# Depthwise-convolution taps in a hybrid SSD / conformer / HGRN2 layer pair: another density, at most two at a step, over a longer stretch of the program

## The chip, the cores and the metric

The program runs on one NeuronCore of a Trainium2 chip. The core has TensorE (PE in the rows; PEld is its weight load), VectorE (DVE), ScalarE (ACT), GpSimd (POOL) and SyncE (SP, which here issues weight loads). Each engine takes its own instructions strictly in the order in which they were written, and engines wait for each other by semaphores. The metric is the device time of one execution in microseconds (us), the median of several.

## What is computed

Two layers over 256 latent tokens and 256 context tokens of width 1024. Layer 0 has a combined input projection, a Mamba-2 scan in both directions beside a conformer convolution, one output projection and a mixture of experts; layer 1 has a gated recurrence (HGRN2) and another mixture of experts. The change lies in layer 0. What it moves is the conformer convolution, and around it stand the scan, its gate z and the output projection:

```python
def conformer_conv(v, gate, dw_w, dw_b, ln_g, ln_b, rows):
    u = v * jax.nn.sigmoid(gate)
    ...
    u = dwconv(u, dw_w, dw_b).reshape(b, n, ch)          # 31 taps, 1024 channels
    return jax.nn.silu(layernorm(u, ln_g, ln_b))

    # even_mixer
    o_ssd = ssd_readout(ys_l[0] + ys_l[1], xs_l, pl[..., :SSD_INNER], d_skip, ssd_g)
    o_cf = conformer_conv(pl[..., cf0:cf0 + CF_CH], pl[..., cf0 + CF_CH:], cf_w, cf_b, cf_lng, cf_lnb, rows)
    y_lat = (jnp.concatenate([o_ssd, o_cf.astype(o_ssd.dtype)], axis=-1) @ w_out).astype(hl.dtype)
```

## The kernel before

Channels lie on the 128 partitions in the input projection, so the 1024 conformer channels are eight blocks of 128, and a block holds all 512 tokens in its free dimension. A product of fp32 precision is made of three products of fp32r pieces: a weight piece is split by ScalarE (the high part, L478) and GpSimd or VectorE (the low part, L479) into a buffer `wb`, and a GEMM of one block takes 24 matmuls of 512 columns.

Blocks 0 to 4 of the conformer convolution run on TensorE. Blocks 5, 6 and 7 run on VectorE: `cf_evac` (L691) multiplies value and sigmoid gate into a padded tile `u` (L702, L703), and then puts 31 closures into the list `bgq`, one for each tap. A tap is one instruction of 572 columns on two accumulators `ca`: taps 0 and 1 are tensor-scalar products (L717, L719), taps 2 to 30 are `SCALAR_TENSOR_TENSOR` (L721), and the last one is followed by the two additions (L724, L725) that write the block's output `co[i]`, a quarter of a tile `um`. In all that is 93 taps and six additions.

Three stages of the program follow each other here.

- **The fill.** `states()` and `tiles_of()` run the scan as Python generators that interleave: `group(t, g)` makes the decay matrices `sb` (ScalarE L1093, GpSimd L1090), TensorE sums them, ScalarE takes the exponential `seg` (L1110), VectorE and GpSimd multiply it by `cb` into `sc` (L1117), and TensorE adds `y`. `states()` adds chunk states `S` (GpSimd L1056, VectorE L1060), `rest()` adds the carried part (VectorE `t` L1159, GpSimd `um` L1161). Between these, the list `FILL` writes the GEMMs of conformer blocks 5 to 7 and of the modulation.
- **The end of the recurrence.** When `FILL` is used up, `drain()` steps the generators until none is left, with no GEMM between them.
- **The z gates.** Eight GEMMs make z; `z_gate` (L1217) takes SiLU (ScalarE L1220), multiplies by the scan's result (VectorE L1225, four instructions), scales into the fp32r pair (ScalarE L1227, VectorE L1228), and squares for the norm (ScalarE L1231, GpSimd L1232). ScalarE's split of the weights of later z blocks (L478) stands in the same queue behind these. After the z gates TensorE sums the eight `co` blocks with `ones` (L1419, tile `y`) for the layer norm, and starts the output projection.

What sets the order of the taps is `step(us, rate)`. Each call runs the generators once, adds `us * rate` to a credit, capped at 6.0, and then writes one tap from `bgq` for each whole unit of credit. `cm_gemm` calls it twice for a GEMM, with 3.8 and 1.9 us, `mod_task` twice with 1.7 us. `RATE[0]` is 1.4 in the fill and in the z gates, and `drain()` calls `step()` without time, so it adds no credit. What is left in `bgq` is written behind the last z GEMM.

Of the kernel before, what the change touches and what calls it, by code (L numbers as in the profile page):

```python
# [89 lines left out]
def build(tc, I, out):  # L90
# [32 lines left out]

    live, pend = [], []
    bgq = []
    credit = [0.0]

    def begin(g):
        live.append(g)

    def step(us=0.0, rate=0.0):

        todo = list(pend)
        pend.clear()
        for f in todo:
            f()
        for g in list(live):
            if next(g, live) is live:
                live.remove(g)
        credit[0] = min(credit[0] + us * rate, 6.0)  # L140
        while credit[0] >= 1.0 and bgq:
            bgq.pop(0)[1]()
            credit[0] -= 1.0

    def drain():
        n = 0
        while live or pend:
            step()
            n += 1
            assert n < 500  # L150

# [7 lines left out]
    class Slots:  # L159
# [27 lines left out]
        def main(self, *a):  # L187

            n = 0
            while (x := self.now(*a)) is None:  # L190
                n += 1
                assert n < 500
                step()
            return x
# [287 lines left out]
    class Pieces:  # L482
# [26 lines left out]
        def next(self, keep=False):  # L509

            if not keep:
                self.release()
            self.ahead()
            v, r, b = self.ready.pop(self.pos)
            self.pos += 1
            self.held.append((r, b))
            return v
# [139 lines left out]
    cfp = stcf.enter_context(tc.tile_pool(name="cfp", bufs=1))  # L657


    RATE = [0.6]  # L660

    def bg(us):
        step(us, RATE[0])

# [162 lines left out]
    def mod_task(l, b, slots=ACC):  # L827
        acc = slots.main()
        for kh in range(2):
            mod_half(acc.ap, l, b, kh)  # L830
            bg(1.7)

        def g():
            sb = yield from TMP.take()
            SC.activation(sb.ap, acc.ap, AF.Copy)
            acc.done()
            yield
            p = yield from TRS.take()
            mod_cols(p.ap, sb.ap)
            sb.done()  # L840
            yield
            mod_add(p.ap, l, b)
            p.done()
            mods_done.add((l, b))
        pend.append(lambda: begin(g()))
# [143 lines left out]
    for i in range(8):  # L989
# [4 lines left out]
        for b in CF_AT.get(i, ()):  # L994
            cf_task(b)
    drain()
    stcf.close()
    st1.close()
# [179 lines left out]
    def tiles_of(pace):  # L1178
        n = 0
        for t in range(4):  # L1180
            begin(cb(t))
            for g in range(4):
                begin(group(t, g))
                nlive[0] += 1
                if g % 2:
                    begin(rest(t, g // 2))
                for _ in range(pace):
                    yield
                while nlive[0] > 3:
                    yield  # L1190

    begin(states())
    begin(tiles_of(3))
    RATE[0] = 1.4
    for f in FILL:
        if f[0] == "cvg":
            if f[2]:
# [2 lines left out]
                cm_task(lambda acc: PA.update(v=acc))  # L1200
        else:
            mod_task(f[1], f[2])
    drain()
    stack_s.close()


# [45 lines left out]
        flags.add("rso")  # L1252

    flags = set()
    RATE[0] = 1.4
    for i in range(8):
        cm_task(lambda acc, i=i: begin(z_gate(i, acc)))
    begin(z_norm())
# [247 lines left out]
    for part in (0, 1):  # L1506
# [4 lines left out]
        for hf in range(2):  # L1511
# [24 lines left out]
            if part == 0 and hf == 1:  # L1536
                uo[0:4] = [unit(og, f"uo{i}") for i in range(4)]
                S.ring(uo[0:4], last=mod_last)
    drain()
    S.hold(True)  # L1540
    P.release()
# [1328 lines left out]
```

## Time and profile before

| | us |
|---|---|
| Median of 3 runs | 1563.47 |
| Lowest and highest | 1562.69, 1569.62 |
| Profiled execution | 1567.05 |
| Its span, first to last instruction | 1565.2 |

The page gives for the whole span TensorE 88% busy, VectorE 60%, ScalarE 48%, GpSimd 42%. These are averages over stages with different limits. The stages of the change lie between 280 and 530 us of the span: the fill from the first tap at about 280 to the last `sc` of it at 396.6, the end of the recurrence to 434.5, where the first z GEMM starts, the z gates to 482.4, then the output projection. How to read the rows: a line of the timeline gives start, length, engine, line, operation and tiles, the count, and in brackets the idle time ahead of it and what ended it. A line of groups gives the count, the busy time and mean length in ns, and behind the second bar the idle time ahead with its releaser.

### The profile page before, as it was taken

What the parts mean: (1) busy time and instruction counts of PE and PEld (TensorE: products, weight loads), DVE (VectorE), ACT (ScalarE), POOL (GpSimd) and SP (SyncE); (2) the same over time, 40 slices, a digit from 0 to 9 for tenths busy, and PEclk for the clock granted to TensorE, in tenths of its full rate; (3) what the DMA queues carried; (4) which work ended last, traced back from release to release, by engine and by line L of the source; (5) the groups of instructions that cost most, each with busy time, mean ns of one, the idle gap of its engine ahead of it and who ended that gap; (6) DMA issues with size and microseconds to landing.
All of it is one profiled execution on the core that took longest, in us unless ns stands there. A gap on an engine that the chain in (4) does not pass through costs nothing. (4 is left out here: it accounts for less than half of the span.)

```text
span 1565.2 us, 19174 instructions
## 1 busy us (share of the span) xinstructions
PE 1383.8 (88%) x7144; PEld 920.0 (59%) x7144; DVE 937.0 (60%) x1268; ACT 755.2 (48%) x1269; POOL 653.7 (42%) x408
## 2 busy tenths in 40 slices
PE   5999989796698988799999994799999988999995
PEld 2677755454476665576666772677777765433432
DVE  2665540899397466789999882634645655132223
ACT  4453435363535534578887882644444553212222
POOL 4333324787855374356667552333233324000000
PEclk9999999898899999899999997799999998999998
DMA  9266443553024164899999995422212466899994
GB/s 332 86 153 153 121 117 135 162 189 107 2 66 150 54 215 155 292 372 374 373 373 333 346 372 210 164 82 79 80 56 81 170 261 273 366 420 420 420 421 172
DMA packets 154311, 340.56 MB, mean 218 GB/s; under 512 B 8105, under 2 KB 45233, under 8 KB 141408
## 3 DMA queue, kind: packets, MB, share of 16 engines
q1 hardware_dynamic: 147440, 323.69, 58.2%
q0 software_dynamic: 5504, 11.79, 2.4%
q10 hardware_dynamic: 1264, 3.73, 0.7%
q8 instruction: 61, 1.00, 0.3%
q14 instruction: 42, 0.34, 0.1%
HBM read 332.79 MB, written 12.42 MB: 221 GB/s over the span
## 5 line engine op out<-in xcount | busy, mean ns | idle before, releaser
L479 POOL TENSOR_TENSOR wb<-wring,wb 128x1024 fp32r<-128x1024 f32 x68 | 170.1, 2504 | 275.4 <-ACT wb L478 232.5
L99 PE MATMUL acc<-hh,wb 128*128 128x512 f32 x640 | 207.3, 401 | 4.0 <-ACT wb L478 2.1
L478 ACT ACTIVATE wb<-wring 128x1024 fp32r<-128x1024 f32 x90 | 94.8, 1058 | 104.0 <-PE acc L99 57.3
L99 PEld LDWEIGHTS acc<-hh,wb 128*128 128x128 f32 x640 | 119.2, 188 | 39.1 <-issue 6.0
L99 PE MATMUL acc<-wb,um 128*96 128x512 f32 (+1 forms) x480 | 122.8, 402 | 5.9 <-DVE wb L479 2.9
L99 PE MATMUL acc<-hl,wb 128*128 128x512 f32 x320 | 126.9, 396 | 0.3 <-DVE hl L604 0.2
L721 DVE SCALAR_TENSOR_TENSOR ca<-u,pcol,ca 128x572 f32<-128x572 f32 x87 | 109.7, 1318 | 0.0
L99 PEld LDWEIGHTS acc<-wb,um 128*96 128x96 f32 (+1 forms) x480 | 79.2, 169 | 38.7 <-DVE wb L479 6.0
L99 PE MATMUL y<-hu,hu 128*64 128x512 f32 (+2 forms) x296 | 85.0, 519 | 4.6 <-DVE hu L2167 2.7
L2611 POOL DMA_INDIRECT hu<-hD,ig x7 | 7.1, 1010 | 172.4 <-DVE ig L2610 154.4
L479 POOL TENSOR_TENSOR um<-wring,um 128x1024 fp32r<-128x1024 f32 x17 | 53.8, 3166 | 55.3 <-ACT um L478 53.1
L2659 DVE TENSOR_TENSOR sg<-sg,y 64x512 f32<-64x512 f32 x16 | 11.1, 692 | 106.8 <-ACT sg L2658 106.8
L99 PE MATMUL acc<-um,um 128*96 128x512 f32 (+2 forms) x272 | 69.1, 394 | 2.8 <-POOL um L479 2.8
L99 PEld LDWEIGHTS acc<-hl,wb 128*128 128x128 f32 x320 | 60.1, 188 | 15.2 <-DVE hl L604 1.6
L479 DVE TENSOR_TENSOR wb<-uo,wb 128x1024 fp32r<-128x1024 f32 x32 | 60.6, 1928 | 9.8 <-ACT wb L478 9.5
L99 PE MATMUL acc<-uo,um 128*96 128x512 f32 (+1 forms) x240 | 62.9, 400 | 0.0
L479 POOL TENSOR_TENSOR um<-uo,um 128x1024 fp32r<-128x1024 f32 x18 | 50.2, 2790 | 26.4 <-ACT um L478 26.3
L873 DVE SCALAR_TENSOR_TENSOR xa<-xin,pcol,xa 128x514 f32<-128x514 f32 x64 | 58.7, 918 | 2.3
L2658 ACT ACTIVATE sg<-y 64x512 f32<-64x512 f32 x16 | 9.4, 588 | 104.3 <-PE y L99 104.3
L99 PEld LDWEIGHTS y<-hu,hu 128*64 128x64 f32 (+2 forms) x296 | 31.5, 150 | 39.5 <-issue 33.6
L99 PEld LDWEIGHTS acc<-um,um 128*96 128x96 f32 (+1 forms) x272 | 43.6, 176 | 17.8 <-POOL um L479 5.7
L99 PE MATMUL acc<-wb,hxh 128*128 128x512 f32 x160 | 52.7, 411 | 0.0
(672 smaller groups left out, 3477.5 us busy)
## 6 DMA issues: line engine op xcount, KB each, us to landing
wring<-in_mod_w_dram SPq DMA_DIRECT2D x32, 1024.0 KB, 5.3
uo<-in_moe_w_down_dram SPq DMA_DIRECT2D x19, 1024.0 KB, 14.4
wring<-in_moe_w_gate_dram SPq DMA_DIRECT2D x16, 1024.0 KB, 13.7
hu<-in_moe_w_gate_dram SPq DMA_DIRECT2D x16, 1024.0 KB, 14.5
uo<-in_moe_w_up_dram SPq DMA_DIRECT2D x13, 1024.0 KB, 9.9
wring<-in_moe_w_up_dram SPq DMA_DIRECT2D x13, 1024.0 KB, 8.4
wring<-in_hg_w_in_dram SPq DMA_DIRECT2D x13, 1024.0 KB, 5.2
hu<-in_moe_w_down_dram SPq DMA_DIRECT2D x13, 1024.0 KB, 10.5
```

What stands on the lines that cost most here:

```text
L99: PE.matmul(o, l, r, start=start, stop=stop, skip_group_check=True)
L478: SC.activation(hv, w, AF.Copy)
L479: eng.tensor_tensor(lv, w, hv.bitcast(F32), op=ALU.subtract)
L721: DV.scalar_tensor_tensor(a, x, w, a, op0=ALU.mult, op1=ALU.add)
L873: DV.scalar_tensor_tensor(a[:, 0:514], x[:, k:k + 514], par("sc_w", 16 * k + i), a[:, 0:514], op0=ALU.mult, op1=ALU.add)
L2611: GP.indirect_dma_start(out=xg1[0:n], out_offset=None, in_=hD1[:, :], in_offset=bass.IndirectOffsetOnAxis(ap=ig[0:n, :1], axis=0), bounds_ ...
L2658: SC.activation(sv[up], av[0:CAP], AF.Silu)
L2659: DV.tensor_tensor(sv[up], sv[up], av[up], op=ALU.mult)
```

## The change

`RATE[0]` goes from 1.4 to 0.7 in both places, `step` writes at most two taps in a call, and the `drain` behind the fill gets 1.5 us for each of its steps, so that it writes taps too. Nothing else changes: the same 93 taps and six additions, the same instructions on all engines.

```diff
     live, pend = [], []
     bgq = []
+    RATE = [0.6]
     credit = [0.0]
...
         credit[0] = min(credit[0] + us * rate, 6.0)
-        while credit[0] >= 1.0 and bgq:
+        n = 0
+        while credit[0] >= 1.0 and bgq and n < 2:
             bgq.pop(0)[1]()
             credit[0] -= 1.0
-
-    def drain():
+            n += 1
+
+    def drain(us=0.0):
         n = 0
         while live or pend:
-            step()
+            step(us, RATE[0])
             n += 1
             assert n < 500
...
-    RATE = [0.6]
...
-    RATE[0] = 1.4
+    RATE[0] = 0.7
     for f in FILL:
...
-    drain()
+    drain(1.5)
     stack_s.close()
...
     flags = set()
-    RATE[0] = 1.4
+    RATE[0] = 0.7
     for i in range(8):
         cm_task(lambda acc, i=i: begin(z_gate(i, acc)))
```

The order of instructions on TensorE, ScalarE, GpSimd and SyncE is the same in both kernels; only VectorE's differs. Three places of it follow. Line numbers are three higher in the kernel after up to L660, and two higher behind it.

VectorE in the last part of the fill, before: `S`, `sc` and `t` are the instructions that TensorE and GpSimd wait for, `ca` are the taps.

```order
L1073 TENSOR_TENSOR cb_2571<-acc_2572,mL 128x512
L721 SCALAR_TENSOR_TENSOR ca<-u,pcol,ca 128x572 x2
L1117 TENSOR_TENSOR sc<-seg,cb_2570 128x512
L436 TENSOR_REDUCE modc_166<-tr 128x8
L437 TENSOR_TENSOR modc_166<-modc_166,pcol 128x8
L721 SCALAR_TENSOR_TENSOR ca<-u,pcol,ca 128x572 x3
L1060 TENSOR_TENSOR S<-S,acc_2641 128x512
L721 SCALAR_TENSOR_TENSOR ca<-u,pcol,ca 128x572 x7
L1117 TENSOR_TENSOR sc<-seg,cb_2570 128x512
L1159 TENSOR_TENSOR t_2744<-acc_2720,sm_439 128x512
```

The same place after:

```order
L1075 TENSOR_TENSOR cb_2551<-acc_2552,mL 128x512
L723 SCALAR_TENSOR_TENSOR ca<-u,pcol,ca 128x572 x2
L1119 TENSOR_TENSOR sc<-seg,cb_2550 128x512
L439 TENSOR_REDUCE modc_166<-tr 128x8
L440 TENSOR_TENSOR modc_166<-modc_166,pcol 128x8
L723 SCALAR_TENSOR_TENSOR ca<-u,pcol,ca 128x572 x2
L726 TENSOR_TENSOR um_101<-ca 128x256
L727 TENSOR_TENSOR um_101<-ca 128x256
L1062 TENSOR_TENSOR S<-S,acc_2617 128x512
L719 TENSOR_SCALAR ca<-u,pcol 128x572
L721 TENSOR_SCALAR ca<-u,pcol 128x572
L723 SCALAR_TENSOR_TENSOR ca<-u,pcol,ca 128x572
```

Where 3 and 7 taps stood ahead of `S` and of `sc`, two stand now, with the end of block 5 and the two opening taps of block 6.

VectorE at the end of the recurrence, before:

```order
L1117 TENSOR_TENSOR sc<-seg,cb_2902 128x512 x2
L1159 TENSOR_TENSOR t_2996<-acc_2987,sm_439 128x512
L1159 TENSOR_TENSOR t_3027<-acc_3007,sm_439 128x512
L1117 TENSOR_TENSOR sc<-seg,cb_2902 128x512 x2
L1159 TENSOR_TENSOR t_3095<-acc_3086,sm_439 128x512
L1159 TENSOR_TENSOR t_3109<-acc_3106,sm_439 128x512
L721 SCALAR_TENSOR_TENSOR ca<-u,pcol,ca 128x572 x13
L1225 TENSOR_TENSOR uo_3125<-uo_3125,um_102 128x128 x2
```

The same place after:

```order
L1119 TENSOR_TENSOR sc<-seg,cb_2873 128x512
L723 SCALAR_TENSOR_TENSOR ca<-u,pcol,ca 128x572 x4
L1119 TENSOR_TENSOR sc<-seg,cb_2873 128x512
L1161 TENSOR_TENSOR t_2973<-acc_2963,sm_439 128x512
L723 SCALAR_TENSOR_TENSOR ca<-u,pcol,ca 128x572 x2
L1161 TENSOR_TENSOR t_3006<-acc_2985,sm_439 128x512
L723 SCALAR_TENSOR_TENSOR ca<-u,pcol,ca 128x572
L1119 TENSOR_TENSOR sc<-seg,cb_2873 128x512
L723 SCALAR_TENSOR_TENSOR ca<-u,pcol,ca 128x572 x3
L1119 TENSOR_TENSOR sc<-seg,cb_2873 128x512
L1161 TENSOR_TENSOR t_3078<-acc_3068,sm_439 128x512
L723 SCALAR_TENSOR_TENSOR ca<-u,pcol,ca 128x572 x2
```

Taps now stand between the last `sc` and `t`, where none stood; 16 of them in this stretch.

VectorE at the last two z gates, before (`uo_3125` holds z, `A_170` is a gain that is needed later):

```order
L1225 TENSOR_TENSOR uo_3125<-uo_3125,um_103 128x128 x2
L1228 SCALAR_TENSOR_TENSOR uo_3124<-uo_3125,pcol,uo_3122 128x512
L1225 TENSOR_TENSOR uo_3125<-uo_3125,um_102 128x128 x2
L1225 TENSOR_TENSOR uo_3125<-uo_3125,um_103 128x128 x2
L457 SCALAR_TENSOR_TENSOR A_170<-modc_166,pcol 128x16
```

The same place after (`um_101` holds the blocks 4 to 7 of the convolution's output):

```order
L1227 TENSOR_TENSOR uo_3113<-uo_3113,um_103 128x128 x2
L723 SCALAR_TENSOR_TENSOR ca<-u,pcol,ca 128x572 x2
L1230 SCALAR_TENSOR_TENSOR uo_3112<-uo_3113,pcol,uo_3110 128x512
L723 SCALAR_TENSOR_TENSOR ca<-u,pcol,ca 128x572 x2
L1227 TENSOR_TENSOR uo_3113<-uo_3113,um_102 128x128 x2
L1227 TENSOR_TENSOR uo_3113<-uo_3113,um_103 128x128 x2
L723 SCALAR_TENSOR_TENSOR ca<-u,pcol,ca 128x572 x4
L726 TENSOR_TENSOR um_101<-ca 128x256
L727 TENSOR_TENSOR um_101<-ca 128x256
L460 SCALAR_TENSOR_TENSOR A_170<-modc_166,pcol 128x16
```

Each of the first six gates now has two taps between its products and its L1228 and two behind that, and block 7 ends behind the seventh gate's products instead of ahead of the third's.

## Rows read from the trace of the kernel before

**Rows 1.** The page's first line: span and instructions.

```profile
span 1565.2 us, 19174 instructions
```

**Rows 2.** Stages: stretch, its length, busy PE, PEld, DVE, ACT, POOL, PEclk, DMA.

```profile
280.00:396.60 116.60, 88.77 (x504) 56.30 (x504) 112.28 (x116) 53.26 (x136) 95.84 (x76) 0.89 0.46 145
396.60:434.50 37.90, 28.22 (x177) 19.84 (x178) 12.16 (x18) 18.18 (x55) 28.81 (x27) 0.89 0.00 0
434.50:482.40 47.90, 45.82 (x197) 36.02 (x195) 44.56 (x54) 19.04 (x26) 27.56 (x12) 1.00 0.34 104
```

**Rows 3.** Waits of TensorE from 280 to 400 us: total us, times, longest.

```profile
PE y L99 <- DVE sc L1117: 10.2, 3, 5.4
PE acc L99 <- DVE S L1060: 5.1, 2, 3.9
...
PE y L99 <- DVE modc L436: 1.7, 1, 1.7
```

**Rows 4.** Timeline of TensorE in the fill.

```profile
349.82 1.10 PE L99 MATMUL y<-sc,xd 128*64 128x128 f32 x16
...
382.61 1.98 PE L99 MATMUL y<-sc,xd 128*64 128x128 f32 x16 [3.87 <-DVE sc L1117]
384.51 2.08 PE L99 MATMUL acc<-S,um 128*128 128x256 f32 x4
```

**Rows 5.** Groups of VectorE in the fill, 280 to 396.6 us.

```profile
L721 DVE SCALAR_TENSOR_TENSOR ca<-u,pcol,ca 128x572 f32<-128x572 f32 x61 | 80.8, 1381 | 0.0
```

**Rows 6.** Line L721 alone: shortest, median and longest tap in ns.

```profile
L721 DVE SCALAR_TENSOR_TENSOR ca<-u,pcol,ca x87: 793/1157/3011, 282.1 to 462.1; 128x572 f32<-128x572 f32 x87
```

**Rows 7.** Groups of GpSimd in the fill, 280 to 396.6 us.

```profile
L1105 POOL TENSOR_TENSOR xd<-um,sm 128x256 f32<-128x256 f32 x18 | 17.5, 993 | 0.0
...
L1090 POOL TENSOR_TENSOR sb1h<-mL,lah 128x512 fp32r<-128x512 f32 x9 | 13.3, 1483 | 0.0
...
L1161 POOL TENSOR_TENSOR um<-um,t 128x512 f32<-128x512 f32 x6 | 9.3, 1543 | 15.7 <-DVE t L1159 15.7
```

**Rows 8.** Groups of GpSimd at the recurrence's end, 396.6 to 434.5 us.

```profile
L1161 POOL TENSOR_TENSOR um<-um,t 128x512 f32<-128x512 f32 x6 | 8.1, 1352 | 2.2 <-DVE t L1159 2.2
...
L1105 POOL TENSOR_TENSOR xd<-um,sm 128x256 f32<-128x256 f32 x9 | 6.7, 762 | 0.0
L1090 POOL TENSOR_TENSOR sb1h<-mL,lah 128x512 fp32r<-128x512 f32 x4 | 4.2, 1038 | 0.0
```

**Rows 9.** Groups of VectorE at the recurrence's end, 396.6 to 434.5 us.

```profile
L1159 DVE TENSOR_TENSOR t<-acc,sm 128x512 f32<-128x512 f32 x6 | 4.1, 689 | 7.1 <-PE acc L99 7.1
L1117 DVE TENSOR_TENSOR sc<-seg,cb 128x512 f32<-128x512 f32 x5 | 3.6, 712 | 15.3 <-ACT seg L1110 15.3
```

**Rows 10.** Timeline of VectorE in the z gates.

```profile
431.43 14.82 DVE L721 SCALAR_TENSOR_TENSOR ca<-u,pcol,ca 128x572 f32<-128x572 f32 x13
446.17 0.88 DVE L1225 TENSOR_TENSOR uo<-uo,um 128x128 f32<-128x128 f32 x4
...
469.55 3.84 DVE L1225 TENSOR_TENSOR uo<-uo,um 128x128 f32<-128x128 f32 x4 [0.25 <-ACT uo L1220]
474.24 0.75 DVE L1228 SCALAR_TENSOR_TENSOR uo<-uo,pcol,uo 128x512 fp32r<-128x512 f32 x1 [0.86 <-ACT uo L1227]
475.24 3.88 DVE L1225 TENSOR_TENSOR uo<-uo,um 128x128 f32<-128x128 f32 x4 [0.25 <-ACT uo L1220]
```

**Rows 11.** Timeline of GpSimd in the z gates.

```profile
469.11 1.31 POOL L1232 TENSOR_TENSOR uo<-uo 128x512 f32<-128x512 f32 x1 [2.50 <-ACT uo L1231]
470.54 2.50 POOL L479 TENSOR_TENSOR wb<-wring,wb 128x1024 fp32r<-128x1024 f32 x1
```

**Rows 12.** Timeline of TensorE where the z gates end.

```profile
482.44 1.92 PE L99 MATMUL y<-um,ones 128*32 128x512 f32 x16
...
486.15 1.64 PE L99 MATMUL acc<-wb,uo 128*128 128x512 f32 x6
491.62 1.12 PE L469 MATMUL tr<-ident,modc 128*128 128x128 f32 x4 [3.83 <-ACT m2r L471]
```

## The prediction, made before the changed kernel was run

> **What bounds the kernel now.** I first read the span [rows 1] and then the stages around the moved taps [rows 2]. In the fill (280 to 396.6 us) VectorE is busy 112.28 of 116.6 us, GpSimd 95.84 and TensorE only 88.77, at a granted clock of 0.89. At the end of the recurrence (to 434.5) VectorE does 12.16 of 37.9 us, while GpSimd works 28.81. In the z gates TensorE is busy 45.82 of 47.9 at a clock of 1.00, and VectorE 44.56. So VectorE paces the fill, then stands nearly idle for a stage, and then is full again.
>
> The waits of TensorE in the fill [rows 3] name the instructions behind which it stands: `sc` 10.2 us, `S` 5.1, `modc` 1.7, together 17.0. None of these is long itself; they stand behind taps in VectorE's queue. 61 of the `SCALAR_TENSOR_TENSOR` taps run there at a mean of 1381 ns [rows 5]; with the six opening taps 67 of the 93 stand in the fill, and no row shows VectorE idle ahead of a tap. GpSimd waits for the same queue: 15.7 us ahead of its `um` for VectorE's `t` [rows 7]. Each long wait costs TensorE twice: the `y` products behind the 3.87 us wait took 1.98 us where the same sixteen took 1.10 elsewhere, and the next products 2.08 [rows 4], the mark of the lower of the two clock levels.
>
> **The fill.** Counted in the order of instructions, 40 taps stand in it after instead of 67, and at most four in a row instead of seven (most often two). 27 taps less at 1.381 us are 37 us of VectorE's 112.28, which leaves about 75 us of work: it is no longer the fullest engine. What can TensorE gain? Its waits are 17.0 us, and the low clock cost at most 88.77 x (1 - 0.89) = 9.8 us: 26.8 us if all of it went. What is late next is GpSimd, whose order is unchanged. It was idle 116.6 - 95.84 = 20.8 us in the fill, 15.7 of them behind `t`. Without quicker operations it can't end the stage more than 20.8 us sooner. I take **-18**, between 15.7 and 20.8, nearer to the first, since seven or so of the awaited instructions still find two taps ahead. If each of these cost the mean of one tap, 7 x 1.4 = 10 us of the 17.0 would stay, and with a little of the clock the gain would be 10. Bounds: -10 to -21.
>
> **The end of the recurrence.** 16 taps come here, 18.5 us at the median of 1157 ns [rows 6]. VectorE's idle time here is 15.3 us ahead of `sc` and 7.1 ahead of `t` [rows 9], and the taps stand in front of just these, four, two, one, three, two at a time, so for VectorE they mostly fit. They aren't free for GpSimd, though. The same operations on GpSimd are longer where VectorE is full: `sb1h` 1483 ns in the fill against 1038 here, `xd` 993 against 762, `um` 1543 against 1352 [rows 7, 8]. With the counts here that is 4 x 0.445 + 9 x 0.231 + 6 x 0.191 = 5.0 us if VectorE were as full as in the fill (96%). It goes from 32% to (12.16 + 18.5) / 37.9 = 81%, some three quarters of the way: 3.8 us. GpSimd is on the path here (28.81 of 37.9 busy, ScalarE's `seg` the other link), so I count **+4**. Bounds: 0 (its 9.1 us of idle time takes it in) to +9 (every one of 16 taps holds GpSimd up for its shortest 0.793 us, 12.7, less some of that idle time).
>
> The rows show GpSimd slowed beside VectorE, not stopped. The Trainium skill, "SBUF — State Buffer", section "Who interferes with whom", says that a VectorE instruction with two SBUF inputs contends with a GpSimd instruction that reads SBUF, and that one holds the port pair for its whole length while the other blocks. By that rule the sum would use the upper bounds here and in the next part.
>
> **The z gates.** I count from E, the start of the first z GEMM (434.5 before). Before, VectorE starts 13 taps at E - 3.1 and they take 14.82 us, 1.14 each [rows 10]. After, it has six taps and the two additions of block 6, then the two opening taps and one more of block 7: 7 x 1.14 + some 3.1 = 11.1, so the first gate's products start at E + 8.0 and end at E + 8.9 [0.88, rows 10], sooner than at 446.17 (E + 11.7) before. Then come six gates with four taps each. A gate without taps repeats every 5.69 us (469.55 to 475.24), of which 3.84 are the products, held up while GpSimd splits weights from 470.54 for 2.50 us [rows 10, 11]. That is the floor of a gate with taps. The ceiling is all in turn: VectorE 0.88 + 0.75 + 4 x 0.793 = 4.8, GpSimd 1.31 + 2.50 = 3.8 [rows 6, 10, 11], together 8.6. I take the middle, 7.2: the seventh gate's products end at E + 8.9 + 6 x 7.2 = E + 52.1. Four taps and two additions follow, 5.8 us: block 7 is ready at E + 57.9.
>
> Who waits for it? Before, block 7 ended ahead of the third gate. Now TensorE, in order, stands at the sums `y<-um,ones`, which it reached before at 482.44, E + 47.9 [rows 12], and behind these the output projection is queued. So this is a new wait of some 10 us. But TensorE stood at that place before as well: after two units of the output projection (1.64 each) it waited 3.83 us for ScalarE's `m2r` and went on only at 491.62, E + 57.1 [rows 12]. After, it goes on at E + 57.9 with the last of the sums (1.0), the two units (3.3) and the small ones still to do, some 4.4 us: 57.9 + 4.4 - 57.1 = **+5**. With a gate of 5.7 us the taps end 9 us sooner and the term is about -2 (the gates' own waits of TensorE, 47.9 - 45.82 = 2.1, go too); with 8.6 it is +14.
>
> **The sum.** -18 + 4 + 5 = -9 us. The profiled execution took 1567.05 us, with a span of 1565.2 [rows 1], and lies 3.6 above the median of 1563.47. 1567.05 - 9 = 1558; taken to the median, 1563.5 - 9 = **1554.5 us**. Behind 500 us nothing is changed, and no row says that a shift of 9 us would be lost.
>
> **The rivals.**
> - *The taps hide almost entirely* (-21 in the fill, 0 at the recurrence's end, -2 in the gates): -23, 1540 us. For it speaks VectorE's idle time of 15.3 and 7.1 us [rows 9]; against it the 3.84 us for products that take 0.88 alone [rows 10].
> - *GpSimd and ScalarE take over the fill.* Taps stay in front of the awaited instructions and GpSimd's 95.84 of 116.6 us hardly shrink: -10 + 4 + 5 = -1, 1562.5 us, no change. For it speaks that GpSimd is nearly as full as VectorE; against it, that 15.7 us of its idle time hang on `t`.
> - *Slower: block 7 becomes the end of the stage.* VectorE and GpSimd take turns, a gate needs 8.6 us, block 7 comes at E + 66.3, the gates cost +14, the recurrence's end +9, and the fill brings only 10: +13, 1576 us. With -10 and +4 for the other two, it decides from a gate of some 8.6 us on (-10 + 4 + 14 = +8). The page's rule named above would give this case; the trace agrees with it where one split stops the products (3.84 against 0.88), not in the fill, where both engines show over 80% busy.
> - *The change doesn't do what it says.* The order shows that it does; 0.02.
>
> **How the numbers follow.** Forecast within 5 us of 1554.5: 0.44. Hidden: 0.16. Fill taken over: 0.28. Slower: 0.10. A measurement of this kernel can tell about 0.5%, 7.8 us, from no change. Faster by more than that (below 1555.7) are all of the hidden case and about two thirds of the forecast, 0.46; within it the rest of the forecast and the third case, 0.45; slower 0.09. The range reaches from within the hidden case (1543) to 4 us above now (1567.5), which leaves out most of the slower case and a part of the hidden one.
>
> **What would show it.** In the profile after, TensorE's waits for `sc` and `S` in the fill should fall from 15.3 to under 6 us, its clock there rise from 0.89, and GpSimd's 15.7 us ahead of `um` shrink to a few. At the recurrence's end `sb1h` and `xd` should be longer than 1038 and 762 ns. In the gates the products L1225 should follow each other by about 7 us, and `y<-um,ones` should show a wait for VectorE of about 10 us, which the row before doesn't have. I am wrong if the fill is less than 10 us shorter, or if a gate repeats under 6 or over 8.5 us.

## The result, and the profile after

| | before | after |
|---|---|---|
| Median of 20 runs each, us | 1563.78 | 1555.05 |
| Ratio after / before, 95% interval | | 0.9929 [0.9916, 0.9941] |
| Span of the profiled execution | 1565.2 | 1552.2 |
| Fill: first tap to TensorE's last `y<-sc` of the stage | 116.4 | 93.7 |
| End of the recurrence, to the first z GEMM (E) | 37.6 | 43.7 |
| z gates, E to `rso` on VectorE | 67.8 | 73.6 |
| Block 7's last addition ends | E + 32.6 | E + 59.4 |

The kernel is 0.7% faster, 1555.05 against a forecast of 1554.5 us. One of the 20 executions after took 1966.87 us at a mean clock of 0.648; it counts in the median (1554.63 without it), and the ratio leaves it out. The stages come from the starts of four instructions in the timelines of one profiled execution each. They changed by -22.7, +6.1 and +5.8, together -10.8 us; the other 2.2 us of the span lie ahead of the first tap (-1.2) and behind `rso` (-1.0). The medians differ by 8.7 us and the profiled executions by 13.1, since the one before lay 3.3 us above its median and the one after 1.1 below.

The page's first line of the kernel after:

```profile
span 1552.2 us, 19176 instructions
```

The three stages after, with the columns of [rows 2]:

```profile
279.10:372.80 93.70, 80.52 (x504) 53.17 (x505) 77.75 (x85) 49.79 (x126) 85.22 (x73) 0.96 0.56 180
372.80:416.50 43.70, 29.02 (x176) 20.18 (x177) 37.16 (x36) 21.34 (x66) 39.69 (x30) 0.88 0.00 1
416.50:462.70 46.20, 46.20 (x194) 37.12 (x194) 43.05 (x53) 19.05 (x26) 26.71 (x12) 0.97 0.38 114
```

In the fill VectorE (third of the busy times) fell from 112.28 to 77.75 us and is no longer the fullest engine: GpSimd is, 85.22 of 93.7. TensorE's clock rose from 0.89 to 0.96. At the end of the recurrence VectorE and GpSimd, which did 12.16 and 28.81 us, are now busy for 37.16 and 39.69 of 43.7.

TensorE's waits in the fill after, 279 to 376 us, which answer to [rows 3] (total us, times, longest):

```profile
PE acc L99 <- DVE u L705: 2.4, 2, 1.4
PE y L99 <- DVE modc L439: 2.3, 1, 2.3
PE y L99 <- DVE sc L1119: 2.3, 2, 1.2
PE y L99 <- POOL um L1163: 2.2, 3, 1.0
PE acc L99 <- DVE S L1062: 2.1, 1, 2.1
PE y L99 <- POOL sc L1119: 1.8, 2, 1.4
PE acc L99 <- POOL xd L1043: 1.5, 2, 1.3
PE tr L99 <- POOL sb1h L1092: 0.3, 1, 0.3
```

The waits for `sc` and `S` went from 15.3 to 4.4 us. No wait is longer than 2.3 us, and four of the eight lines name GpSimd (POOL), with 5.8 of 14.9 us. GpSimd's groups in the fill after, which answer to [rows 7]:

```profile
L1107 POOL TENSOR_TENSOR xd<-um,sm 128x256 f32<-128x256 f32 x16 | 13.8, 878 | 0.0
...
L1092 POOL TENSOR_TENSOR sb1h<-mL,lah 128x512 fp32r<-128x512 f32 x8 | 11.3, 1411 | 0.0
...
L1163 POOL TENSOR_TENSOR um<-um,t 128x512 f32<-128x512 f32 x6 | 9.4, 1567 | 4.2 <-DVE t L1161 4.2
```

Its idle time behind `t` went from 15.7 to 4.2 us; `xd` went from 993 to 878 ns and `sb1h` from 1483 to 1411, while `um` stayed as it was (1543 and 1567). At the end of the recurrence, which answers to [rows 8], the same instructions went the other way, `um` from 1352 ns, `xd` from 762 and `sb1h` from 1038:

```profile
L1163 POOL TENSOR_TENSOR um<-um,t 128x512 f32<-128x512 f32 x6 | 10.1, 1686 | 2.6 <-DVE t L1161 2.6
L1107 POOL TENSOR_TENSOR xd<-um,sm 128x256 f32<-128x256 f32 x10 | 9.3, 953 | 0.0
L1092 POOL TENSOR_TENSOR sb1h<-mL,lah 128x512 fp32r<-128x512 f32 x5 | 7.2, 1444 | 0.0
```

One gate of the kernel after, VectorE's timeline (start, length); [rows 10] showed gates without taps:

```profile
450.83 0.88 DVE L1227 TENSOR_TENSOR uo<-uo,um 128x128 f32<-128x128 f32 x4
451.64 1.53 DVE L723 SCALAR_TENSOR_TENSOR ca<-u,pcol,ca 128x572 f32<-128x572 f32 x2
453.09 0.74 DVE L1230 SCALAR_TENSOR_TENSOR uo<-uo,pcol,uo 128x512 fp32r<-128x512 f32 x1
453.75 4.72 DVE L723 SCALAR_TENSOR_TENSOR ca<-u,pcol,ca 128x572 f32<-128x572 f32 x2
458.39 0.89 DVE L1227 TENSOR_TENSOR uo<-uo,um 128x128 f32<-128x128 f32 x4
```

GpSimd in the same gate:

```profile
453.13 1.85 POOL L1234 TENSOR_TENSOR uo<-uo 128x512 f32<-128x512 f32 x1 [2.83 <-ACT uo L1233]
454.95 2.91 POOL L482 TENSOR_TENSOR wb<-wring,wb 128x1024 fp32r<-128x1024 f32 x1
```

The two pairs are the same instructions. The first runs while GpSimd stands idle and takes 1.53 us; the second runs beside GpSimd's sum of squares and weight split and takes 4.72, to 0.6 us behind the split's end. A gate repeats after 7.56 us, and VectorE has no idle time in it. TensorE at the end of the z gates, which answers to [rows 12]:

```profile
463.26 1.92 PE L99 MATMUL y<-um,ones 128*32 128x512 f32 x14
475.93 1.91 PE L99 MATMUL y<-um,ones 128*32 128x512 f32 x2 [10.76 <-DVE um L727]
```

Here is the forecast wait of some 10 us, for the second addition of block 7.

### The profile page after: what moved, and what is told of

The parts are those of the page before. It is cut to its first block, busy times and chain, and to the rows that moved or that the text cites. A ratio compares the mean times of both kernels' runs of the same rounds, so it can differ in the third digit from the quotient of the medians.

```text
span 1552.2 us, 19176 instructions
## 1 busy us (share of the span) xinstructions
PE 1372.9 (88%) x7144; PEld 915.8 (59%) x7144; DVE 937.1 (60%) x1268; ACT 755.0 (49%) x1269; POOL 655.6 (42%) x408
## 5 line engine op out<-in xcount | busy, mean ns | idle before, releaser
L2661 DVE TENSOR_TENSOR sg<-sg,y 64x512 f32<-64x512 f32 x16 | 11.1, 692 | 106.8 <-ACT sg L2660 106.8
```

The costliest lines, as they stand in the source:

```text
L2661: DV.tensor_tensor(sv[up], sv[up], av[up], op=ALU.mult)
```

## The experiments

All ratios are to the kernel before. The stages are cut as in the table above; "rest" is what lies behind `rso`. "One-input" kernels have other instructions in place of taps (below).

| kernel | fill | end | gates | rest | span | ratio, 95% interval |
|---|---|---|---|---|---|---|
| before | 116.4 | 37.6 | 67.8 | 1063.1 | 1565.2 | |
| after | 93.7 | 43.7 | 73.6 | 1062.1 | 1552.2 | 0.9929 [0.9916, 0.9941] |
| limit of two alone | 101.1 | 39.2 | 78.9 | 1061.5 | 1558.1 | 0.9986 [0.9969, 1.0003] |
| density of the fill alone | 92.6 | 39.2 | 83.1 | 1065.4 | 1558.1 | 0.9958 [0.9943, 0.9973] |
| after, no taps at the end | 93.6 | 36.5 | 88.8 | 1065.2 | 1561.8 | 1.0001 [0.9984, 1.0017] |
| after, no taps of block 7 | 93.8 | 43.2 | 61.0 | 1061.4 | 1539.1 | 0.9858 [0.9813, 0.9903] |
| after, sums later | 93.8 | 42.8 | 72.8 | 1067.8 | 1554.9 | 0.9951 [0.9934, 0.9968] |
| after, end at 2.2 us a step | 93.8 | 50.0 | 67.0 | 1062.8 | 1552.1 | 0.9938 [0.9917, 0.9959] |
| after, end at 3.0 us a step | 93.1 | 56.8 | 61.8 | 1063.1 | 1556.5 | 0.9934 [0.9911, 0.9957] |
| after, end taps one-input | 93.4 | 37.9 | 73.9 | 1059.2 | 1543.4 | 0.983 [0.9803, 0.9856] |
| after, gate taps one-input | 93.1 | 43.7 | 62.1 | 1055.7 | 1532.9 | 0.9806 [0.9786, 0.9826] |
| after, fill taps one-input | 84.5 | 43.5 | 73.7 | 1056.0 | 1535.4 | 0.9838 [0.9814, 0.9862] |
| after, sums in PSUM | 124.5 with the end | | 67.1 | 1065.1 | 1536.4 | 0.9834 [0.981, 0.9858] |
| the same, end at 2.2 us a step | 127.4 with the end | | 60.4 | 1060.1 | 1528.2 | 0.9818 [0.9795, 0.9841] |

The rest differs by up to 8 us between kernels that compute the same (1060.1 to 1067.8). In the three "one-input" kernels, whose convolution output is another, it is 3 to 6 us below the kernel after, and the ratios of all three lie 0.4 to 0.5% below the ranges that I expected. What does that was not settled, so a mechanism is read from its stage and not from the ratio.

### Which part of the change shortens the fill?

**The limit of two taps a step alone**, on the kernel before:

```diff
-        while credit[0] >= 1.0 and bgq:
+        n = 0
+        while credit[0] >= 1.0 and bgq and n < 2:
...
+            n += 1
```

> The kernel before with the limit of two taps at a step and nothing else: rate 1.4 in the fill and the gates, no taps at the recurrence's end. 52 of the 93 taps stand in the fill (before 67, after 40), 35 in the gates, 11 of them in one block behind the seventh gate. Theory A, the number of taps in front of the awaited instructions sets the fill: 15 taps fewer of the 27 that the change takes out give 15/27 of its 22.7 us, with the shorter blocks some more, 13 to 18 us off the fill; the recurrence's end stays at 37.6 us; block 7 ends some 8 us later than in the change, so the gates cost 13 instead of 6. Sum about -2 us, ratio 0.997 to 1.001. Theory B, only the length of a block of taps matters (seven ahead of one sc): the fill gains its full 22 us, ratio 0.992 to 0.995.

The ratio was 0.9986, theory A. 15 taps left the fill and shortened it by 15.3 us; they came back in the gates (+11.1) and at the recurrence's end (+1.6).

**The density of the fill alone**, on the kernel before:

```diff
     begin(tiles_of(3))
-    RATE[0] = 1.4
+    RATE[0] = 0.7
```

> The kernel before with the rate 0.7 in the fill alone: no limit at a step, no taps at the recurrence's end, rate 1.4 in the gates. As many taps leave the fill as in the change; the gates get 13 taps ahead of the first and then eight a gate, with the end of block 7 ahead of the seventh gate's products. Theory A: the fill from the first tap to the last y of it takes about 94 us as in the change (116.4 before), the recurrence's end 37.6 as before, and the gates up to the norm's rso about 85 instead of 67.8, since TensorE waits at the sums of the convolution for block 7 some 20 us. Sum -23 + 0 + 17 = -6 us, ratio 0.996. Theory B (the block length alone): blocks of three are left, the fill gains half, the ratio is over 1.0.

The ratio was 0.9958, and the fill 92.6 us, as short as in the kernel after without any limit on a step. So the lower number of taps gives the gain by itself, and the limit adds nothing to it: 27 fewer are worth 22.7 us, 0.84 each. What the length of a row of taps costs isn't separated by this, since at half the density the rows get shorter too (mostly one to three taps, where there were up to eight). The first 15 taps to leave, which left with shorter rows, were worth 1.02 us each and the other 12 some 0.6.

### What do the taps cost where they went?

**No taps at the end of the recurrence**: `drain()` in place of `drain(1.5)`, on the kernel after.

> The kernel after without taps at the recurrence's end (its drain adds no credit): the fill as in the change, the 16 taps go behind the gates, 25 in one block behind the seventh. Theory A, the end of the recurrence is 6 us longer in the change (43.7 against 37.6 us) because taps on VectorE slow GpSimd: it falls back to 37.6 here; block 7 comes some 17 us later, so the gates to rso take about 90 instead of 73.6. Sum -23 + 0 + 23 = 0, ratio 0.998 to 1.002. Rival: the end of the recurrence is longer because it starts in another state (shorter fill, GpSimd behind), then it stays at 42 to 44 us and the ratio is 1.002 to 1.006.

The end of the recurrence went back to 36.5 us and the gates grew to 88.8; the whole gain of the change was gone (1.0001). TensorE's wait at the sums, in this kernel's timeline:

```profile
483.05 1.92 PE L99 MATMUL y<-um,ones 128*32 128x512 f32 x2 [25.64 <-DVE um L727]
```

The 16 taps of the prediction are those between the end of the fill and the last `t`. In VectorE's order this edit moves 21: ahead of the first gate's products there are 44 instead of 65, and behind the seventh gate's 25 in one row instead of four. So 21 taps cost 7.2 us at the end (43.7 - 36.5), 0.34 each; behind the last gate, where nothing covers them, they cost 15.2 (88.8 - 73.6), 0.72 each.

**No taps of block 7**: 28 of its 31 are left out of the kernel after.

```diff
         def tap(k):
             def f():
+                if i == 7 and 2 <= k < 30:
+                    return
```

> The kernel after with taps 2 to 29 of block 7 left out (that block's output is then only two taps and the last); fill and recurrence's end are the change's own. Theory A, the gates cost 6 us because block 7 is late at TensorE's sums: the 10.8 us wait ahead of the sums goes, the gates follow each other in 5.7 us, and the stretch from the first z GEMM to rso takes about 66 us instead of 73.6. Sum -11 - 7.5 = -18 us against before, ratio 0.987 to 0.990. Rival: the wait at the sums only covers the wait for m2r that stood there before, then a wait of 4 us or more shows at m2r again, and the ratio is over 0.991.

The sums no longer wait for block 7. The gates took 61.0 us, 12.6 less; I had expected 66, since TensorE would then stand at `m2r` as before [rows 12]. That wait shrank too, to 0.8 us: `m2r` stands behind the gates in ScalarE's queue and came at E + 51.1, where it came at E + 56.7 before, since the gates ended sooner.

**More taps at the end**, on the kernel after: `drain(2.2)`, ten more, and `drain(3.0)`, nineteen more.

> The kernel after with 2.2 instead of 1.5 us of credit at each step of the recurrence's end: ten more taps stand there and ten fewer in the gates, and block 7 ends behind the fifth gate's products. A tap has cost 0.4 us at the recurrence's end (6.1 us for 16) and about as much in the gates as long as block 7 is late. Theory A: the end of the recurrence takes 48 us instead of 43.7, the wait at the sums goes, the gates to rso take about 66 instead of 73.6; ratio 0.990 to 0.992. Rival: VectorE is too full there and sc and t are late behind three and five taps: 51 us or more, ratio 0.993 to 0.996.

> The kernel after with 3.0 us of credit at each step of the recurrence's end: 19 more taps there, blocks of four and six in front of sc and t, nine taps left in the gates. Theory A with 0.4 us a tap: 51 to 52 us for the recurrence's end, about 62 us for the gates to rso, ratio 0.990 to 0.992. Rival: VectorE becomes the limit there as it was in the fill before, each further tap costs its full 0.8 to 1.2 us: 58 us or more, ratio 0.994 to 0.997.

Both came nearer to my rival than to my theory: its ratios were 0.993 to 0.996 and 0.994 to 0.997, its ends 51 and 58 us or more. The ten added 6.3 us at the end (0.63 each) and took 6.6 off the gates; the nineteen added 13.1 (0.69 each) and took 11.8. I had 0.4 (6.1 us over sixteen taps); the first 21 had cost 0.34. Between end and gates there was nothing left to win by moving taps.

**The sums later**, so that the output projection's first units would stand ahead of TensorE's wait, on the kernel after (in the generator of the layer norm):

```diff
         while None in co:
             yield
+        for _ in range(3):
+            yield
```

> The kernel after with three more steps ahead of TensorE's sums of the convolution, so that three units of the output projection stand in front of them instead of behind. Theory A, the wait of 10.8 us at the sums holds up work that needs no block 7: some 5 us of it are filled, the wait falls to 5 or 6 us, ratio 0.989 to 0.991. Rival, the layer norm's chain on VectorE and ScalarE is as late as the sums and ends just ahead of the second half of the output projection: what is won at the sums is lost there, ratio 0.992 to 0.995.

0.9951: my theory of a gain fell. The gates won 0.8 us where I had expected some 5, and the wait was moved, not removed. Two of the three units were done when TensorE stood for `m2r` instead:

```profile
476.73 1.12 PE L472 MATMUL tr<-ident,modc 128*128 128x128 f32 x4 [9.88 <-ACT m2r L474]
```

In ScalarE's queue `m2r` stands behind two DMA issues (L1271) into tiles of a pool that is opened where the pool of `u` and `ca` is closed. Here they start at 472.56 us, and the last addition of block 7 ends at 472.47; in the kernel after the two are 475.96 and 475.88, without block 7's taps 464.31 and 464.23. So ScalarE, too, goes on only behind block 7. That the tiles share the memory is read from the code and these times; no run here separates it. Behind `rso` the profiled run is longer by 5.7 us, within what the rest differs anyway.

### Why does a tap cost what it does?

A tap reads two SBUF tiles, `u` and `ca`. The next three kernels write in its place a `TENSOR_REDUCE` over the 602 columns of `u`, which has one SBUF input, each in one stage only (`inend` is set around that stage):

```diff
                 elif k == 1:
                     DV.tensor_scalar(a, x, w, None, op0=ALU.mult)
+                elif inend[0] and k < 30:
+                    DV.tensor_reduce(junk, u, axis=AX.X, op=ALU.add)
```

**At the end of the recurrence:**

> The kernel after, where each tap written at the recurrence's end is replaced by a reduction over the 602 columns of the same tile u into one column: about as long on VectorE, at the same place in its queue, with one input in SBUF instead of two. Those taps are left out of the result. Theory A, the end of the recurrence is 6 us longer because two-input taps slow GpSimd: it falls from 43.7 to 38 to 39.5 us, and sb1h and xd on GpSimd go back towards 1038 and 762 ns; ratio 0.988 to 0.990. Rival, sc and t are late because they stand behind a tap in VectorE's queue: the stretch stays at 42 to 44 us with GpSimd's operations short, ratio 0.992 to 0.994.

37.9 us against 43.7, though the same number of instructions stands in the same places of VectorE's queue. GpSimd's groups there (371 to 410 us):

```profile
L1112 POOL TENSOR_TENSOR xd<-um,sm 128x256 f32<-128x256 f32 x12 | 8.5, 730 | 0.0
L1168 POOL TENSOR_TENSOR um<-um,t 128x512 f32<-128x512 f32 x6 | 7.6, 1270 | 2.3 <-DVE t L1166 2.3
L1097 POOL TENSOR_TENSOR sb1h<-mL,lah 128x512 fp32r<-128x512 f32 x5 | 5.2, 1041 | 0.0
```

These are the lengths of [rows 8] again. Four taps in a row of the kernel after, and the four reductions at the same place:

```profile
386.18 5.49 DVE L723 SCALAR_TENSOR_TENSOR ca<-u,pcol,ca 128x572 f32<-128x572 f32 x4
```

```profile
385.85 3.21 DVE L726 TENSOR_REDUCE junk<-u 128x1 f32<-128x602 f32 x4
```

1.37 us each against 0.80. The rival, that VectorE's queue alone delays what stands behind, falls. How much of the 5.8 us comes through GpSimd's shorter instructions, and how much through `sc` and `t` behind shorter taps, the run doesn't divide.

A reduction also writes one column where a tap writes 572, so the write could be the cause in place of the second input. The trace of the kernel after speaks against that: VectorE's `t` has one input in SBUF (`acc` lies in PSUM) and writes 512 columns to SBUF, and all twelve took 677 to 692 ns from 279 to 416.5 us, seven of them wholly inside an instruction of GpSimd. `sc`, with two inputs in SBUF, took 676 to 1755 ns. One `t`, and GpSimd at that time:

```profile
382.41 0.68 DVE L1161 TENSOR_TENSOR t<-acc,sm 128x512 f32<-128x512 f32 x1
```

```profile
381.84 1.55 POOL L1092 TENSOR_TENSOR sb1h<-mL,lah 128x512 fp32r<-128x512 f32 x1
```

**In the z gates:**

> The kernel after, with taps 2 to 29 that are written during and behind the z gates (some 33 of them) replaced by one-input reductions over the tile u (602 columns, 0.79 us each where GpSimd is busy); the convolution's last blocks are thus not computed. Theory A (in a gate the second pair of taps stands behind GpSimd's squares and weight split, 4.72 us for two in the kernel after, where the first pair takes 1.53): the second pair takes some 1.6 us, a gate repeats after 5.7 to 6.2 us instead of 7.6, the products of the seventh end near E + 44, block 7 is ready by E + 49, and TensorE's 10.8 us wait at the sums falls under 3. Gates to rso 61 to 64 instead of 73.6, the time 10 to 12 us less, ratio to the kernel before 0.985 to 0.988. Rival (the number of instructions that stand between the products of two gates sets the period, whatever they read): the gates stay 7 us or longer, the wait over 6 us, ratio 0.990 to 0.993.

Theory A held. One gate on VectorE, and GpSimd beside it:

```profile
442.52 0.89 DVE L1232 TENSOR_TENSOR uo<-uo,um 128x128 f32<-128x128 f32 x4
443.32 1.59 DVE L726 TENSOR_REDUCE junk<-u 128x1 f32<-128x602 f32 x2
444.82 1.76 DVE L1235 SCALAR_TENSOR_TENSOR uo<-uo,pcol,uo 128x512 fp32r<-128x512 f32 x1
446.51 1.58 DVE L726 TENSOR_REDUCE junk<-u 128x1 f32<-128x602 f32 x2
448.01 0.89 DVE L1232 TENSOR_TENSOR uo<-uo,um 128x128 f32<-128x128 f32 x4
```

```profile
443.63 2.42 POOL L482 TENSOR_TENSOR wb<-wring,wb 128x1024 fp32r<-128x1024 f32 x1 [1.38 <-ACT wb L481]
446.00 1.74 POOL L1239 TENSOR_TENSOR uo<-uo 128x512 f32<-128x512 f32 x1
```

Both pairs take 1.6 us, the first beside GpSimd's split and the second beside its sum, and the split takes 2.42 us in place of 2.91. The gate repeats after 5.49 us. What still waits is L1235, which has two SBUF inputs: 1.76 us, where it took 0.74 without GpSimd. TensorE's wait at the sums fell to 1.52 us, and the gates to 62.1.

**In the fill**, where the question was what bounds it by now:

> The kernel after, with taps 2 to 29 that are written in the fill (35 of 40) replaced by the same one-input reductions; two of the convolution's blocks are thus not computed. It asks what still bounds the fill. Theory A (GpSimd, held up by the taps): with the mean lengths that its instructions have at the end of the recurrence in the kernel before, its 85.2 busy us become some 79, sb1h falls from 1411 ns to under 1150, and the fill from 93.7 to 86 to 89 us; ratio 0.989 to 0.991 (0.9929 for the kernel after). Rival (TensorE, busy 80.5 of 93.7 us, and ScalarE's exponentials set the fill by now; the taps that are left are hidden): GpSimd's instructions are shorter all the same, but the fill stays at 92 to 94, ratio 0.992 to 0.994.

Theory A, and further than expected: 84.5 us. The fill (columns of [rows 2]), and two groups of GpSimd (278 to 365 us):

```profile
277.80:362.20 84.40, 76.78 (x504) 51.44 (x505) 54.72 (x85) 49.24 (x123) 72.14 (x73) 1.00 0.63 199
```

```profile
L1112 POOL TENSOR_TENSOR xd<-um,sm 128x256 f32<-128x256 f32 x17 | 11.0, 667 | 0.0
L1097 POOL TENSOR_TENSOR sb1h<-mL,lah 128x512 fp32r<-128x512 f32 x9 | 9.8, 1093 | 0.0
```

GpSimd's 73 instructions took 72.14 us where the same number took 85.22, and TensorE's mean clock is 1.00. So what the 33 replaced taps (of the 40 still in the fill) cost as two-input instructions is 9.2 us. That they cost it through GpSimd fits these lines but isn't shown alone: VectorE's own work fell too, from 77.75 to 54.72 us.

### A version that follows from it

If the second SBUF input is the price, the sum can live elsewhere. In this kernel, which computes everything, each block takes one PSUM bank from the accumulator list `ACC` of TensorE for its life; a tap is then two instructions of 256 columns that read `u` from SBUF and the sum from PSUM, and the last one writes the output:

```diff
+                if k == 0:
+                    pa[0] = ACC.now()
+                if pa[0] is not None:
+                    p = pa[0].ap
+                    d = o if k == 30 else p
+                    r = lambda z: z[:, 256:512].rearrange("p (r c) -> p r c", c=64)
+                    for y, x, z in ((d[:, 0:256], u[:, k:k + 256], p[:, 0:256]), (r(d), rows79(u, 271 + k), r(p))):
+                        if k == 0:
+                            DV.tensor_scalar(y, x, w, par("cf_b", i), op0=ALU.mult, op1=ALU.add)
+                        else:
+                            DV.scalar_tensor_tensor(y, x, w, z, op0=ALU.mult, op1=ALU.add)
...
```

> The kernel after with the whole computation, but each block on VectorE sums its taps in one PSUM bank (held from the bank list of TensorE's accumulators for the life of the block) instead of two SBUF tiles: a tap is two instructions of 256 columns with one SBUF input (u) and one PSUM input, the last tap writes the output. Theory A (a tap costs what it does because its two SBUF inputs hold GpSimd up and are held up by it): as with the reductions, sb1h is near 1040 to 1100 ns in fill and recurrence's end, a pair of taps in a gate takes 1.7 us even beside GpSimd's weight split, the fill is 85 to 90 us (the accumulator taken from TensorE's list moves its order there, which may cost some), the recurrence's end 37 to 39, the gates to rso 61 to 64, against 93.7, 43.7 and 73.6: the time 18 to 26 us under the kernel after, ratio to the kernel before 0.976 to 0.982. Rival 1 (the contention is of VectorE with GpSimd as such, or the sum in place waits for itself): taps stay at 1.2 us or more for both halves and the gates over 70: ratio 0.990 to 0.996. Rival 2 (the missing accumulator stalls TensorE in the fill more than the ports give): fill over 94, ratio about 0.985 or more with the gates at 62.

0.9834 [0.981, 0.9858], 1.0% below the kernel after. It lies between the 0.976 to 0.982 that I expected and the second rival's 0.985, and its interval reaches both, so the lengths of instructions and stages decide. VectorE's taps in the gates, and one group of GpSimd in the fill (279 to 363 us):

```profile
433.79 2.06 DVE L726 SCALAR_TENSOR_TENSOR acc<-u,pcol,acc 128x256 f32<-128x256 f32 x4
435.76 0.95 DVE L1247 SCALAR_TENSOR_TENSOR uo<-uo,pcol,uo 128x512 fp32r<-128x512 f32 x1
436.63 2.05 DVE L726 SCALAR_TENSOR_TENSOR acc<-u,pcol,acc 128x256 f32<-128x256 f32 x4
...
450.60 6.26 DVE L726 SCALAR_TENSOR_TENSOR acc<-u,pcol,acc 128x256 f32<-128x256 f32 x12
```

```profile
L1109 POOL TENSOR_TENSOR sb1h<-mL,lah 128x512 fp32r<-128x512 f32 x8 | 8.3, 1038 | 0.0
```

Both pairs of a gate (four instructions now) take 2.05 us, the first beside GpSimd's split and the second beside its sum, and `sb1h` is at its 1038 ns in the fill itself. Fill and end together took 124.5 us, 12.9 less than in the kernel after (one bank fewer moves TensorE's order, so the border between the two isn't the same instruction). The gates took 67.1 and not 61 to 64, for a tap is 1.03 us, not 0.8, and block 7 still comes last:

```profile
457.81 1.76 PE L99 MATMUL y<-um,ones 128*32 128x512 f32 x2 [5.13 <-DVE um L726]
```

**The same with 2.2 us of credit a step at the end**, eight taps more there:

> The kernel with the PSUM accumulator, with more taps at the end of the recurrence (2.2 us of credit a step there instead of 1.5), so that block 7 ends ahead of the products of the seventh gate; all is computed. In the kernel after, ten more taps there cost 0.63 us each and won as much in the gates. Theory A (what a tap cost there was GpSimd held up): the recurrence's end grows by 0 to 2 us only, the gates to rso fall from 67.1 to 61.5 to 63, TensorE's 5.1 us wait at the sums goes: 3 to 6 us less than with 1.5, ratio to the kernel before 0.9795 to 0.982 where the other measured 0.9834. Rival (VectorE's own time ahead of the awaited sc and t is the price, some 0.5 us a tap, whatever the ports): end +4 to +5, gates -5, ratio 0.982 to 0.985, nothing won again.

The wait at the sums is gone (gates 60.4), and the end and fill grew by 2.9 us, 0.36 a tap, between theory (up to 2) and rival (4 to 5): a tap there has a price without the second SBUF input, too. The ratio, 0.9818, can't be told from the 0.9834 of the other: the intervals overlap.

## Why the prediction was right, and where not

**The sum** of -9 came out as -10.8 in the three stages: end +6.1 for +4 and gates +5.8 for +5, both within their bounds, and the fill -22.7 for -18. The direction and the three terms held. That 1554.5 lies within 0.6 us of the median is luck in part: the fill's gain was 4.7 us too small and the two costs 2.9 too small, and the rest is the difference between the profiled executions and the medians.

**The fill was mis-sized**: -22.7 for -18, beyond the bound of -21. The term that failed is the bound itself. I held that GpSimd, with an unchanged order, couldn't end the stage more than its 20.8 us of idle time sooner "without quicker operations". Its operations did get quicker: 95.84 us of work became 85.22 (three of the 76 instructions lie outside the new stretch, some 3 to 4 us of that), and its idle time went from 20.8 to 8.5. So the source that I had named, this idle time, gave 12.3 of the stretch's 22.9 us and not 15.7 to 20.8; quicker instructions gave some 7, and 3 to 4 went over to the next stage. I had priced GpSimd's slowness beside a full VectorE for the end of the recurrence, from the same rows [rows 7, 8], and left it out for the fill, where it has the other sign. The one-input kernel bears this out: without the second input of 33 taps the fill is 84.5.

**What would show it** came as written: `sc` and `S` 4.4 us (under 6), clock 0.96 (above 0.89), GpSimd's wait ahead of `um` 4.2 (a few), `sb1h` and `xd` 1444 and 953 ns at the end, a gate every 7.56 us (about 7; the sum used 7.2), 10.76 us at `y<-um,ones` (about 10).

**Why a gate takes 7.56 us** I had as a middle between two bounds, for want of a row. The gate shows it: VectorE's own work, 0.88 + 1.53 + 0.74 and two taps of 0.77, is 4.7 us; the other 2.9 are the second pair standing behind GpSimd. With one-input instructions in its place the gate took 5.49.

**The rule of the Trainium skill** that I weighed ("SBUF — State Buffer", section "Who interferes with whom": a VectorE instruction with two SBUF inputs and a GpSimd instruction that reads SBUF exclude each other for the length of the one that came first) I let count for the gates only, since in the fill both engines showed over 80% busy. That reading was wrong: the busy time of either engine contains its standing. Two rows of the fill after show it, VectorE's and GpSimd's. The instruction has two inputs in SBUF, and the shortest of its kind took 0.17 us:

```profile
365.91 1.02 DVE L440 TENSOR_TENSOR modc<-modc,pcol 128x8 f32<-128x8 f32 x1
```

```profile
365.12 1.78 POOL L1163 TENSOR_TENSOR um<-um,t 128x512 f32<-128x512 f32 x1
```

An instruction of eight columns takes 1.02 us, and ends at 366.93, with GpSimd's at 366.90. So the trace agrees with the rule in the fill as well. The trace of the kernel before had held such a row, where GpSimd's `um` and then a weight split ran (349.01 to 350.69 and on):

```profile
351.47 2.10 DVE L437 TENSOR_TENSOR modc<-modc,pcol 128x8 f32<-128x8 f32 x1
```

It doesn't follow that the bounds all in turn were the ones to use: the gate came to 7.56, not 8.6, so about 1 us of the two engines' work did overlap. Where in the gate was not found.

**The rivals.** That GpSimd takes over the fill was half true: it is the fullest engine there now, and shortening its instructions brought 9.2 us more, but it got 10.6 us lighter by the change itself. That the taps hide almost entirely fell with the kernel without taps at the end: 0.34 us each there. Block 7 did become the last to come in the gates, at a smaller price than the slower case needed. It holds up ScalarE and its `m2r` as well as the sums, which the prediction didn't count.

**Two theories of mine fell** behind the prediction: that the price of the first taps at the end, which I took for 0.4 us, would hold for the next (0.63 to 0.69), and that moving the sums would win the wait back.

## What to carry to other kernels

Before filler work is moved on VectorE, count its SBUF inputs: with two of them it isn't free even where VectorE stands idle, for it holds GpSimd up and GpSimd holds it up, and "busy" in the profile contains that. Look for it by comparing the mean length of the same GpSimd group between stages. Here a sum kept in PSUM brought 1.0% on top of the 0.7% of placing the taps better. And when a price is read from one row for a cost in one stage, use the same row with the other sign where the work was taken away.

## What the chip showed that I had not expected

- An opening tap, `TENSOR_SCALAR` with one SBUF input, is held up as well. On VectorE of the kernel after, two of them of 572 columns followed each other, and GpSimd's weight split stood beside the second:

```profile
357.23 0.57 DVE L719 TENSOR_SCALAR ca<-u,pcol 128x572 f32<-128x572 f32 x1
357.71 2.66 DVE L721 TENSOR_SCALAR ca<-u,pcol 128x572 f32<-128x572 f32 x1
```

```profile
357.35 2.70 POOL L482 TENSOR_TENSOR wb<-wring,wb 128x1024 fp32r<-128x1024 f32 x1 [2.91 <-ACT wb L481]
```

  0.57 us where it started ahead of the split, 2.66 where the split was running, which ended at 360.05. The same section of the Trainium skill counts this operation among those that can use both ports, so one input isn't enough by itself: the reductions and the sums in PSUM aren't held up, this one is.
- A tap on PSUM costs 0.51 us for 256 columns with or without GpSimd beside it (2.05 for four in either pair of a gate, 6.26 for the twelve behind the last), more than half of the 0.77 us of a tap of 572 columns.
